# Beginning two weight units of each late run early in the feed-forward output of an encoder trunk

## The chip, the cores and the metric

The kernel runs on one core of a Trainium2 chip. The metric is the device time of one execution in microseconds (us), lower is better, given as the median of several runs. Engines are named as in the profile: PE is TensorE (matmuls; PEld are its weight loads), DVE is VectorE, ACT is ScalarE, POOL is GpSimd, SP is SyncE, whose queue issues the DMA transfers here.

## The reference

The program computes two layers of an encoder trunk on 512 tokens of 1024 channels. Each layer has a half-step SwiGLU feed-forward, a token mixer (neighbourhood attention in the first layer, a bidirectional RWKV-7 scan in the second) and another half-step feed-forward, each followed by a residual sum and a layer norm. The change touches only the feed-forward:

```
def swiglu(x, w_in, w_out):
    gate, up = jnp.split(x @ w_in, 2, axis=-1)
    return (jax.nn.silu(gate) * up) @ w_out
...
x = layer_norm(DN_ALPHA * x + 0.5 * swiglu(x, ffn_w_in[i, 0], ffn_w_out[i, 0]), ln_g[i, 0], ln_b[i, 0])
```

w_in is 1024 x 5632 and w_out 2816 x 1024, all float32. There are four such layers in the program; below they are called the first, second, third and last.

## The kernel before

**Split products.** A float32 product is made of three matmuls: every operand is split into a high part (`h`, a copy that rounds, on ACT, line 220) and a low part (`l`, the value minus the high part, a subtraction on DVE or POOL, line 221), and high x high, high x low and low x high are summed in PSUM. So each weight unit needs a DMA into a raw buffer, a copy on ACT and a subtraction on DVE or POOL before all of its matmuls can run. The matmul with the high half needs only the copy.

**The output product as a Winograd scheme.** The product with w_out is computed by class `Winograd` (line 753), which replaces eight block products by seven. The 22 chunks of 128 hidden channels form 11 pairs, numbered c = 0 to 10. While the projections of pair after pair run, `sums` makes sums of blocks of w_out, writes two of them (t3 and t4) to a DRAM buffer `late`, and the products X, Z and Y of pair c are accumulated early (`early`, matmuls shown as bank<-wx,an). Four more runs over all 11 pairs follow, made by `add` (matmuls shown as bank<-w,ring or bank<-wl,ring):

- V with block b21 of w_out, pairs 0 to 6 and then 7 to 10;
- t3 into the banks of Y, b22 into the banks of Z, and t4 again into the banks of Y: the three late runs.

A run has 11 pairs x 2 row tiles x 3 matmuls = 66 matmuls. A weight unit holds two pairs (c and c + 1, 128 x 2 x 1024 values after the split), the last one, c=10, holds one. It is loaded by `load` (line 812), when `add` comes to an even c.

**Order of the late runs.** After V the outer function `ffn` opens a pool "fo", makes the 14 additions of X, Y, Z and V into the residual x (`more`, line 446, shown as DVE L448), calls `add` for t3, adds Y for rows 2 and 3, calls `add` for b22, then `done(0)` and `done(1)` (the last addition and the normalisation of rows 0 and 1, lines 359 to 369, then transposes, line 328), then `add` for t4, and the ending of rows 2 and 3. In b22 the pairs from 8 on, and in t4 those from 6 on, are lagging: all of them for row tile 0 first, then all for row tile 1 (`lag`, line 843), so that the first tile is finished sooner.

**Buffers.** A split unit goes into one of three buffers of tag `w`; a unit of lagging pairs into a buffer of its own in the pool "fo": `wl2` (two buffers, units of two pairs) or `wl1` (one buffer, c=10). The trace calls both wl. A `w` or `wl` buffer is free again when PE has done the last matmul that reads it. The raw buffers: the first three loads of a layer take the common raw buffers, the later ones eight quarters of two tiles named `late`, in turn, and, where the next stage takes its input as an XT tile (first and second layer), t4's loads take four buffers `rw`, because the tiles `late` lie in the buffers that the new xT then needs (`out.raws = None`, line 478). Counted over a layer the loads are numbers 0 to 5 for V, 6 to 11 for t3, 12 to 17 for b22 and 18 to 23 for t4; number n takes quarter n % 4 of tile n // 4 % 2.

The low part goes to POOL for c = 0, 4 and 8, and to DVE for c = 2, 6 and 10 (line 828).

**What sets the order.** Outside the hand-ordered sections a planner puts the instructions of each engine in a fixed order at build time: among those that its clock holds ready, the one traced first goes first. On the chip each engine, and SP's queue too, then runs its list in order, and an instruction that waits holds up all behind it. `mark` puts a small copy on POOL, and `behind` queues the next stage's first splits on POOL after it (`ending`, line 252).

Of the kernel before, what the change touches and what calls it, by code (L numbers as in the profile page):

```python
# [86 lines left out]
def halves_of(ap):  # L87
    return ap.rearrange("p (h t) -> p h t", h=2)
# [10 lines left out]
class Trunk:  # L99
    def __init__(self, ctx, tc):  # L100
        self.tc = tc
        self.nc = tc.nc
        self.ex, self.spare = None, []
        self.spares = self.nth = None
        nc = self.nc
        self.const = ctx.enter_context(tc.tile_pool(name="const", bufs=1))
        self.ident = self.const.tile([P, P], F32, name="ident")
        make_identity(nc, self.ident)
        self.eps = self.const.tile([P, 1], F32, name="eps")
        nc.gpsimd.memset(self.eps, LN_EPS)  # L110
        self.marks = self.const.tile([P, 1], F32, name="marks")
# [283 lines left out]
    def ffn(self, xT, w_in, w_out, ln, nxt, lead=None):  # L395

        nc = self.nc
        npairs = NF // 2
        params = self.ln_params(ln)
        out = Winograd(self, w_out)
        with self.pool("fa") as pool:
            out.pool = pool
            keep = [self.ring().rearrange("p (i n s) -> p i n s", i=2, n=4) for _ in range(npairs)]
            for c in range(npairs):
                out.sums(c)  # L410
                raw = pool.tile([P, 8, 256], F32, name="ar", tag="ar", bufs=1)
                for j in range(2):
                    f = 2 * c + j
                    if f == 0:
                        pps = self.follow()
                    elif f >= LEAD // 2:
                        pps = [self.proj_cols(self.load_cols(w_in, FF * i + f * P), xT) for i in range(2)]
                    pg, pu = pps.pop(0), pps.pop(0)
                    s = self.tmp()
                    nc.scalar.activation(s, pg, AF.Silu)  # L420

                    nc.vector.scalar_tensor_tensor(raw[:, 3:7:3] if j else raw[:, 0:8:7], halves_of(pu), 0.5, halves_of(s),  # L422
                                                   ALU.mult, ALU.mult)
                    if j == 0 and c:
                        out.early(c - 1)
                a = lambda n: raw[:, n]
                nc.vector.tensor_tensor(a(1), a(7), a(6), ALU.add)
                nc.vector.tensor_tensor(a(2), a(1), a(0), ALU.subtract)
                nc.gpsimd.tensor_tensor(a(4), a(0), a(7), ALU.subtract)
                nc.gpsimd.tensor_tensor(a(5), a(3), a(2), ALU.subtract)  # L430
                out.now[c] = pool.tile([P, 2, 3, 256], F32R, name="an", tag="an", bufs=1)
                self.split(out.now[c][:, 0], out.now[c][:, 1], raw[:, 0:3])
                self.split(keep[c][:, 0], keep[c][:, 1], raw[:, 3:7])
            out.keep = keep
            late = npairs - 4
            out.raws = [self.sb.tile([P, 4 * D], F32, name="late", tag="xT", bufs=2) for _ in range(2)]
            out.add("V", 0, out.b21, range(0, late))
            out.early(npairs - 1)
            out.add("V", 0, out.b21, range(late, npairs))
        nxt = nxt()  # L440
        with self.pool("fo") as pool:
            out.pool = pool
            fin = self.residual_norm(params, nxt)
            hs = (slice(0, 512), slice(512, 1024))

            def more(t, h, acc, scale=1.0, sm=None):
                y = self.x[t][:, hs[h]]
                nc.vector.scalar_tensor_tensor(y, y, scale, acc[t % 2], ALU.mult, ALU.add, accum_out=sm)  # L448

            X, Y, Z, V = (out.acc[n] for n in "XYZV")  # L450
            st = [self.small("st", 5) for _ in range(NT)]
            for t in (0, 1):
                more(t, 1, Y, ALPHA)
            for t in (2, 3):
                more(t, 1, Z, ALPHA)
            for t in (0, 1):
                more(t, 1, X)
            for t in (2, 3):
                more(t, 1, X)
                more(t, 0, X, ALPHA)  # L460
            for t in (0, 1):
                more(t, 0, X, ALPHA)
                more(t, 0, V, 1.0, st[t][0])
            out.add("Y", 1, out.t3, range(npairs))
            for t in (2, 3):
                more(t, 1, Y, 1.0, st[t][1])
            out.add("Z", 2, out.b22, range(npairs), lag=8)

            def done(t):
                h, acc = (1, Z) if t < 2 else (0, Y)  # L470
                more(t, h, acc, 1.0, st[t][h])
                fin(t, st[t])

            done(0)
            done(1)
            mid = nxt and self.mark(self.x[1][:, 0:1])
            if isinstance(nxt, XT):
                out.raws = None
            out.add("Y", 3, out.t4, range(npairs), lag=6)
            if isinstance(nxt, XT):  # L480

                def start(t):
                    more(t, 0, Y, 1.0, st[t][0])
                    return fin(t, st[t], True)

                self.ending(start, lead, nxt, (mid,), (mid,))
            elif nxt:
                self.mid = mid
                with self.tc.manual_schedule(engines=MANUAL_NORM):
                    more(2, 0, Y, 1.0, st[2][0])  # L490
                    n2 = fin(2, st[2], True)
                    for _ in range(3):
                        next(n2)
                    more(3, 0, Y, 1.0, st[3][0])
                    n3 = fin(3, st[3], True)
                    for n in (n3, n3, n3, n2, n3):
                        next(n)
            else:
                done(2)
                done(3)  # L500
        return nxt
# [251 lines left out]
class Winograd:  # L753


    def __init__(self, k, w):
        self.k, self.nc = k, k.nc
        self.w = w.rearrange("(c j p) f -> p c j f", j=2, p=P)
        self.late = k.late
        self.units, self.now, self.acc, self.loads = {}, {}, {}, 0  # L760

    def sums(self, c):

# [48 lines left out]
    def load(self, src, c, lag):  # L812
        k = self.k
        n = min(2, NF // 2 - c)
        if self.loads < 3:
            raw = k.raw()
        elif self.raws:
            raw = self.raws[self.loads // 4 % 2][:, self.loads % 4 * D : self.loads % 4 * D + D]
        else:
            raw = self.pool.tile([P, D], F32, name="rw", tag="rw", bufs=4)  # L820
        self.loads += 1
        raw = raw[:, : n * 512]
        k.nc.sync.dma_start(raw.rearrange("p (c f) -> p c f", c=n), src(c, n))
        if lag:
            u = self.pool.tile([P, 2, n * 512], F32R, name=f"wl{n}", tag=f"wl{n}", bufs=n)
        else:
            u = k.sb_w.tile([P, 2 * D], F32R, name="w", tag="w", bufs=k.nw)[:, : 2 * n * 512].rearrange("p (i f) -> p i f", i=2)
        k.split(u[:, 0], u[:, 1], raw, k.nc.vector if c % 4 else k.nc.gpsimd)
        return u

    def add(self, name, n, src, cs, lag=None):

        first = self.banks(name)
        step = lambda c, t: self.product(self.acc[name][t], self.keep[c], n, t, us[c], first and c == 0, c == NF // 2 - 1, name != "V")
        us = {}
        for c in cs:
            if c % 2 == 0:
                self.duo = self.load(src, c, lag is not None and c >= lag)
            us[c] = self.duo[:, :, c % 2 * 512 : c % 2 * 512 + 512]
            if lag is None or c < lag:  # L840
                for t in range(2):
                    step(c, t)
        if lag is not None:
            for t in range(2):
                for c in range(lag, NF // 2):
                    step(c, t)
# [130 lines left out]
class Scan:  # L977
# [53 lines left out]
    def receptances(self):  # L1031
# [13 lines left out]
        for hp, i in zip(WR_FIRST, (4, 5, 6, 7)):  # L1045
            load(hp, one(self.units[i][0]))
            if hp == 1:
                for c in range(ND):
                    nc.sync.dma_start(self.xv[:, c, :], self.dram["xv"][:, c, :])
# [643 lines left out]
```

## Time and profile before

| | |
|---|---|
| median of 3 runs | 2267.66 us (2266.18 to 2270.35) |
| the profiled execution | 2262.09 us |
| its span (first to last instruction) | 2260.3 us |
| mean granted TensorE clock | 0.984 |
| DMA | 328.82 MB, mean 145 GB/s |

A row of a timeline gives start and length in us, engine, line, operation, what it writes and reads, the shape, how many instructions are merged, and in brackets the idle time of the engine before it with what ended that. In the view by stages a row gives a stretch, its length, the busy time (and count) of PE, PEld, DVE, ACT and POOL, the granted clock, the DMA share and GB/s. In the waits "<-" names the one waited for. "issue" is time in which the engine waited for nothing that the profile shows. The late runs of the four layers, from the first matmul of V, begin at 300.69, 890.27, 1243.63 and 2185.33 us of the profiled span.

### The profile page before, as it was taken

Reading aid. Unit: us, or ns where it says so; the run is one execution under the profiler, and the core shown is the slowest. Engines: PE = TensorE matmul, PEld = TensorE weight load, DVE = VectorE, ACT = ScalarE, POOL = GpSimd, SP = SyncE. Lnnn points to the kernel's source line nnn. Section 1 sums busy time; section 2 is a strip of 40 time slices with the busy share of each in tenths; the row PEclk is TensorE's granted clock in tenths of the full one; section 3 lists DMA queues with packets and bytes.
Section 4 is the critical chain, followed back from the end, with each engine's and each line's share of the span. In section 5 each row is a group of like instructions: output and inputs, shape, how many; then the busy total and the mean of one; then the engine's idle time right before and its main releaser. Section 6 shows DMA issues by size and latency. Waiting matters only on the chain. (4 is left out here: it accounts for less than half of the span.)

```text
span 2260.3 us, 35130 instructions
## 1 busy us (share of the span) xinstructions
PE 2169.9 (96%) x13784; PEld 1707.2 (76%) x13784; DVE 1084.6 (48%) x1549; ACT 974.6 (43%) x1706; POOL 1423.4 (63%) x1237
## 2 busy tenths in 40 slices
PE   8999999999999999999999988799999898999998
PEld 7888878887888888788888775435666556888886
DVE  2333356376423333743333698435787535233346
ACT  4333335376333333533333436336777533333334
POOL 6878855554487886588777433144776712888763
PEclk9999999999999999999999999899999999999999
DMA  7444463432344445354444534864444542444443
GB/s 204 143 149 145 140 214 101 134 89 91 103 140 149 144 141 181 123 176 140 140 140 134 192 122 143 275 165 132 134 125 119 181 149 85 158 144 140 145 168 121
DMA packets 350497, 328.82 MB, mean 145 GB/s; under 512 B 48458, under 2 KB 277450, under 8 KB 350332
## 3 DMA queue, kind: packets, MB, share of 16 engines
q1 hardware_dynamic: 350332, 326.58, 45.9%
q8 instruction: 108, 1.77, 0.3%
q14 instruction: 57, 0.47, 0.1%
HBM read 262.26 MB, written 47.74 MB: 137 GB/s over the span
## 5 line engine op out<-in xcount | busy, mean ns | idle before, releaser
L221 POOL TENSOR_TENSOR w<-raw,w 128x1024 fp32r<-128x1024 f32 (+2 forms) x203 | 501.5, 2472 | 253.6 <-ACT w L220 240.1
L226 PE MATMUL bank<-xT,w 128*128 128x512 f32 x1416 | 551.8, 390 | 1.7 <-DVE xT L221 1.7
L225 PE MATMUL bank<-xT,w 128*128 128x512 f32 x1416 | 552.9, 390 | 0.0
L227 PE MATMUL bank<-xT,w 128*128 128x512 f32 x1416 | 551.5, 389 | 0.0
L220 ACT ACTIVATE w<-raw 128x1024 fp32r<-128x1024 f32 x207 | 218.4, 1058 | 327.9 <-POOL ts L768 138.0
L422 DVE SCALAR_TENSOR_TENSOR ar<-bank,tmp 128x512 f32<-128x512 f32 x88 | 60.9, 692 | 580.7 <-PE bank L227 566.2
L226 PEld LDWEIGHTS bank<-xT,w 128*128 128x128 f32 x1416 | 266.1, 188 | 56.6 <-DVE xT L221 2.6
L227 PEld LDWEIGHTS bank<-xT,w 128*128 128x128 f32 x1416 | 266.0, 188 | 54.9
L225 PEld LDWEIGHTS bank<-xT,w 128*128 128x128 f32 x1416 | 266.0, 188 | 54.0
L797 PE MATMUL bank<-w,ring 128*128 128x512 f32 x864 | 201.5, 391 | 11.0 <-DVE w L221 10.1
L797 PEld LDWEIGHTS bank<-w,ring 128*128 128x128 f32 x864 | 161.6, 188 | 48.3 <-DVE w L221 13.1
L797 PE MATMUL bank<-wx,an 128*128 128x512 f32 x792 | 187.3, 389 | 0.0
L1360 POOL TENSOR_TENSOR tm<-qs,zs 128x126 f32<-128x126 f32 (+22 forms) x248 | 105.5, 425 | 125.7 <-DVE qs L1353 77.3
L797 PEld LDWEIGHTS bank<-wx,an 128*128 128x128 f32 x792 | 148.8, 188 | 30.8
L221 POOL TENSOR_TENSOR wx<-ra,wx 128x512 fp32r<-128x512 f32 x132 | 166.8, 1291 | 3.5 <-ACT wx L220 2.4
L221 DVE TENSOR_TENSOR ring<-ar,ring 128x1024 fp32r<-128x1024 f32 x44 | 130.0, 2955 | 76.0 <-ACT ring L220 75.9
L420 ACT ACTIVATE tmp<-bank 128x512 f32<-128x512 f32 x88 | 52.6, 598 | 225.8 <-PE bank L227 225.7
L221 POOL TENSOR_TENSOR ring<-raw,ring 128x1024 fp32r<-128x1024 f32 x28 | 69.7, 2499 | 105.6 <-ACT ring L220 105.6
L1362 POOL TENSOR_TENSOR zs<-zs,tm 128x126 f32<-128x126 f32 (+22 forms) x248 | 112.2, 452 | 19.4
L221 POOL TENSOR_TENSOR w<-late,w 128x1024 fp32r<-128x1024 f32 x28 | 71.3, 2547 | 75.9 <-ACT w L220 68.9
L220 ACT ACTIVATE wx<-ra 128x512 fp32r<-128x512 f32 x132 | 82.9, 633 | 72.4 <-PE bank L797 67.9
L225 PE MATMUL bank<-xT,ring 128*128 128x256 f32 (+1 forms) x352 | 104.5, 304 | 9.5 <-ACT xT L220 3.4
(285 smaller groups left out, 3730.5 us busy)
## 6 DMA issues: line engine op xcount, KB each, us to landing
raw<-in_ffn_w_in_dram SPq DMA_DIRECT2D x176, 512.0 KB, 3.7
ra<-in_ffn_w_out_dram SPq DMA_DIRECT2D x44, 1024.0 KB, 4.9
late<-d_late SPq DMA_DIRECT2D x30, 512.0 KB, 6.0
late<-in_ffn_w_out_dram SPq DMA_DIRECT2D x28, 512.0 KB, 4.4
raw<-in_w_qkv_dram SPq DMA_DIRECT2D x24, 512.0 KB, 3.8
d_late<-ts SPq DMA_DIRECT2D x44, 256.0 KB, 3.1
d_late<-ra SPq DMA_DIRECT2D x44, 256.0 KB, 2.0
xs<-ar SPq DMA_DIRECT2D x64, 128.0 KB, 2.3
```

What stands on the lines that cost most here:

```text
L220: self.hi = self.nc.scalar.activation(h, raw, AF.Copy).ins
L221: self.lo = (eng or self.nc.vector).tensor_tensor(l, raw, h.bitcast(F32), ALU.subtract).ins
L225: nc.tensor.matmul(out, wh, xh, start=start, stop=False)
L226: nc.tensor.matmul(out, wh, xl, start=False, stop=False)
L227: nc.tensor.matmul(out, wl, xh, start=False, stop=stop)
L420: nc.scalar.activation(s, pg, AF.Silu)
L422: nc.vector.scalar_tensor_tensor(raw[:, 3:7:3] if j else raw[:, 0:8:7], halves_of(pu), 0.5, halves_of(s), ALU.mult, ALU.mult)
L797: self.nc.tensor.matmul(acc, lhs, u[:, i], start=bool(first) and m == 0, stop=last and m == 2, skip_group_check=more)
L1360: nc.gpsimd.tensor_tensor(tv, qs[:, s, 0:s].rearrange("p (a o) -> p a o", o=1).broadcast_to([P, s, n]), zs[:, s : s + 1, c0:].broadcast_to ...
L1362: nc.gpsimd.tensor_tensor(zs[:, 0:s, c0:], zs[:, 0:s, c0:], tv, ALU.add)
```

## The change

A new method `begin` loads the units c=0 and c=2 of a run ahead of time and keeps them in a table; `add` takes them from there. It is called for t3 as soon as the pool "fo" is open, ahead of the additions; for b22 after t3's products, ahead of the additions of Y to rows 2 and 3; and for t4 after b22's products, ahead of the normalisation of rows 0 and 1 and ahead of `out.raws = None`, so that in the first two layers t4's first two loads use quarters of `late` and only its other four use `rw`. The order of the loads among themselves stays the same. And the unit c=2 of each late run is put into a buffer `wl2` instead of one of `w`: wl2's two buffers now serve, in this order, t3's c=2, b22's c=2 and c=8, and t4's c=2, c=6 and c=8; before they served b22's c=8 and t4's c=6 and c=8.

```
@@ ffn
         with self.pool("fo") as pool:
             out.pool = pool
+            out.begin(out.t3)
             fin = self.residual_norm(params, nxt)
...
             out.add("Y", 1, out.t3, range(npairs))
+            out.begin(out.b22)
             for t in (2, 3):
                 more(t, 1, Y, 1.0, st[t][1])
             out.add("Z", 2, out.b22, range(npairs), lag=8)
+            out.begin(out.t4)
@@ Winograd.load
-        if lag:
+        if lag or c == 2 and src != self.b21:
             u = self.pool.tile([P, 2, n * 512], F32R, name=f"wl{n}", tag=f"wl{n}", bufs=n)
@@ Winograd
+    def begin(self, src):
+        for c in (0, 2):
+            self.begun[src.__name__, c] = self.load(src, c, False)
@@ Winograd.add
             if c % 2 == 0:
-                self.duo = self.load(src, c, lag is not None and c >= lag)
+                now = (src.__name__, c)
+                self.duo = self.begun.pop(now) if now in self.begun else self.load(src, c, lag is not None and c >= lag)
```

More of the change, by code (lines that the diff above doesn't have):

```diff
@@ L442, in ffn @@
             out.pool = pool
+            out.begin(out.t3)
             fin = self.residual_norm(params, nxt)
@@ L464, in ffn @@
             out.add("Y", 1, out.t3, range(npairs))
+            out.begin(out.b22)
             for t in (2, 3):
@@ L467, in ffn @@
             out.add("Z", 2, out.b22, range(npairs), lag=8)
+            out.begin(out.t4)
             def done(t):
@@ L759, in __init__ @@
         self.late = k.late
-        self.units, self.now, self.acc, self.loads = {}, {}, {}, 0
+        self.units, self.now, self.acc, self.loads, self.begun = {}, {}, {}, 0, {}
     def sums(self, c):
@@ L823, in load @@
         k.nc.sync.dma_start(raw.rearrange("p (c f) -> p c f", c=n), src(c, n))
-        if lag:
+        if lag or c == 2 and src != self.b21:
             u = self.pool.tile([P, 2, n * 512], F32R, name=f"wl{n}", tag=f"wl{n}", bufs=n)
@@ L829, in load, with begin @@
         return u
+    def begin(self, src):
+        for c in (0, 2):
+            self.begun[src.__name__, c] = self.load(src, c, False)
     def add(self, name, n, src, cs, lag=None):
@@ L837, in add @@
             if c % 2 == 0:
-                self.duo = self.load(src, c, lag is not None and c >= lag)
+                now = (src.__name__, c)
+                self.duo = self.begun.pop(now) if now in self.begun else self.load(src, c, lag is not None and c >= lag)
             us[c] = self.duo[:, :, c % 2 * 512 : c % 2 * 512 + 512]
```

## The prediction

> **What bounds the kernel now.** I read the page first, then the timeline of PE through the end of each of the four feed-forward layers, then the timelines of VectorE (DVE), GpSimd (POOL) and ScalarE (ACT) at the places where PE stood still. From the page:
>
> ```profile
> PE 2169.9 (96%) x13784; PEld 1707.2 (76%) x13784; DVE 1084.6 (48%) x1549; ACT 974.6 (43%) x1706; POOL 1423.4 (63%) x1237
> ```
>
> TensorE carries the time, so an edit that leaves its work alone can gain only where it idles. The edit touches the end of the feed-forward layers (V, the early products, then the late runs t3, b22 and t4). The timeline of PE there (start, length, count, and in brackets the idle time before and what ended it), first layer:
>
> ```profile
> 300.69 6.06 PE L797 MATMUL bank<-w,ring 128*128 128x512 f32 x26
> ...
> 314.29 8.78 PE L797 MATMUL bank<-w,ring 128*128 128x512 f32 x38
> 324.65 12.53 PE L797 MATMUL bank<-w,ring 128*128 128x512 f32 x54 [1.58 <-DVE w L221]
> 337.72 3.01 PE L797 MATMUL bank<-w,ring 128*128 128x512 f32 x12 [0.54 <-POOL w L221]
> 341.61 8.03 PE L797 MATMUL bank<-w,ring 128*128 128x512 f32 x34 [0.88 <-DVE w L221]
> 349.47 4.24 PE L797 MATMUL bank<-wl,ring 128*128 128x512 f32 x18
> 353.55 8.32 PE L797 MATMUL bank<-w,ring 128*128 128x512 f32 x36
> ...
> 363.75 1.03 PE L328 MATMUL bank<-ident,x 128*128 128x128 f32 x8
> 364.54 5.93 PE L797 MATMUL bank<-wl,ring 128*128 128x512 f32 x25
> ```
>
> The first row gives the pace: 26 matmuls in 6.06 us, the last taking 0.39, so one starts every (6.06 - 0.39) / 25 = 0.227 us. From it to the row of 353.55 (the first of t4) the program has 66 + 18 + 66 + 66 = 216 matmuls (the three matmuls of a split product, by two row tiles, by eleven chunks for V, t3 and b22; 18 early ones), 49.0 us at that pace. The view by stages gives the length of this stretch in each of the four layers, then what PE was busy:
>
> ```profile
> 300.70:353.50 52.80, 49.80 (x217) 40.31 (x216) 34.31 (x39) 22.32 (x23) 26.76 (x11) 1.00 0.58 202
> 890.30:942.90 52.60, 49.78 (x217) 40.31 (x216) 34.57 (x39) 22.28 (x23) 26.62 (x11) 1.00 0.57 202
> 1243.60:1297.00 53.40, 49.64 (x218) 40.45 (x217) 33.20 (x41) 22.30 (x23) 26.23 (x11) 1.00 0.56 199
> 2185.30:2236.50 51.20, 49.74 (x217) 40.46 (x216) 31.41 (x39) 22.42 (x23) 27.23 (x11) 1.00 0.54 188
> ```
>
> Over 49.0 the first three lose 3.8, 3.6 and 4.4 us. In the first they are the three stops of the timeline, 1.58, 0.54 and 0.88, and the other 0.8 is some 0.3 of restart at each. The third and the last layer have other stops:
>
> ```profile
> 1267.59 11.18 PE L797 MATMUL bank<-w,ring 128*128 128x512 f32 x48 [1.58 <-DVE w L221]
> 1280.94 12.11 PE L797 MATMUL bank<-w,ring 128*128 128x512 f32 x52 [2.18 <-DVE w L221]
> ```
>
> ```profile
> 2220.33 12.14 PE L797 MATMUL bank<-w,ring 128*128 128x512 f32 x52 [1.46 <-DVE w L221]
> ```
>
> The last has one stop, 1.46 + 0.3 = 1.8. Together 3.8 + 3.6 + 4.4 + 1.8 = **13.6 us**: this is all that the edit can win there.
>
> **Part by part.**
>
> *Unit c=2 of t3.* What ends the stop at 324.65 is the subtraction (the low half of a split weight) of that unit:
>
> ```profile
> 312.03 1.10 DVE L221 TENSOR_TENSOR w<-late,w 128x512 fp32r<-128x512 f32 x1 [3.50 <-ACT w L220]
> 313.36 7.86 DVE L448 SCALAR_TENSOR_TENSOR x<-x,bank 128x512 f32<-128x512 f32 x13 [0.23 <-PE bank L797]
> ...
> 321.15 3.45 DVE L221 TENSOR_TENSOR w<-late,w 128x1024 fp32r<-128x1024 f32 x1
> ```
>
> ```profile
> 321.12 2.38 POOL L221 TENSOR_TENSOR w<-late,w 128x1024 fp32r<-128x1024 f32 x1 [1.73 <-issue]
> ```
>
> It stands behind 13 additions (L448), and then takes 3.45 us because POOL began unit c=4 just before it. In the last layer the same pair met the other way round, and no stop followed:
>
> ```profile
> 2205.78 1.22 DVE L221 TENSOR_TENSOR w<-late,w 128x1024 fp32r<-128x1024 f32 x1
> ```
>
> ```profile
> 2205.92 3.36 POOL L221 TENSOR_TENSOR w<-late,w 128x1024 fp32r<-128x1024 f32 x1 [1.83 <-issue]
> ```
>
> So 1.22 is its price alone. After the edit its split is asked for ahead of the additions, into wl2, which no late weight holds then, so no matmul of V has to free it. Its source was fetched early:
>
> ```profile
> 298.58 1.41 SPq L823 DMA_DIRECT2D late<-d_late  x3
> ```
>
> ```profile
> DMA to landing us min/median/max: 3.3/5.4/9.5
> ```
>
> The first late loads left by 300.0 and are there by 309.5 at worst. ACT's copy (1.06 us, the rows of w<-late) and DVE's 1.22 fit into the 3.50 us that DVE idles up to 312.03, or just ahead of the additions; PE wants the unit at 314.29 + 38 x 0.227 = 322.9. If the copy waits at the head of ACT's queue, V's last two copies stand behind it, but PE uses their units only after 314.29. Wholly in the additions' way it delays them by 1.2 us (2.4 more if POOL is just ahead); t3's first product, 24 matmuls after 314.29 or at 319.7, needs only the first two, done by 314.8. So it costs nothing while that cover of 5 us lasts. The slot of w that the unit leaves lets c=4 to c=8 be split a turn (12 matmuls, 2.7 us) sooner. Gain 1.9 us in each of the first three layers.
>
> *Units c=0 and c=2 of b22.* What ends the other two stops:
>
> ```profile
> 331.92 2.40 POOL L221 TENSOR_TENSOR wl<-late,wl 128x1024 fp32r<-128x1024 f32 x1 [1.15 <-ACT wl L220]
> 334.34 3.33 POOL L221 TENSOR_TENSOR w<-late,w 128x1024 fp32r<-128x1024 f32 x1
> ```
>
> ```profile
> 335.33 2.88 DVE L221 TENSOR_TENSOR wl<-late,wl 128x512 fp32r<-128x512 f32 x1
> ...
> 338.75 2.81 DVE L221 TENSOR_TENSOR w<-late,w 128x1024 fp32r<-128x1024 f32 x1
> ```
>
> b22's first unit waits on POOL for its own lagging unit c=8; its second waits on DVE behind the lagging c=10 and an addition. The second goes to wl2's other buffer; its source buffer is one of V's last, free at 312.03 + 1.10 = 313.1, and lands 5.4 later, at about 319, long before PE needs it at 341: that stop, 0.88 + 0.3, goes. The first unit still needs a slot of w that t3's c=7 frees, so asking earlier buys little by itself; c=8, its rival on POOL, does come earlier, since t3's c=4 leaves its source buffer 2.7 us sooner. I take half of that stop as gone.
>
> *The last units of t3* make the stop of 2.18 in the third layer and of 1.46 in the last:
>
> ```profile
> 1275.64 2.48 DVE L221 TENSOR_TENSOR wl<-late,wl 128x512 fp32r<-128x512 f32 x1 [6.37 <-ACT wl L220]
> 1278.04 2.84 DVE L221 TENSOR_TENSOR w<-late,w 128x512 fp32r<-128x512 f32 x1
> ```
>
> Unit c=10 of t3 follows b22's c=10 on DVE, each slowed by POOL beside it. b22's lagging source is requested when t3's c=4 and c=6 have been split. That comes about 2.7 us sooner while PE, without its first stop, wants c=10 only 1.9 sooner, so most of this goes too. But the same order can now arise in the first two layers. By these rows a unit of half width, 0.6 us alone by the 1.22 for a whole one, took 2.84: the loser of such a meeting is late by 2.2 us; I take one meeting in four, 0.5 per layer.
>
> The Trainium skill (SBUF — State Buffer, "Who interferes with whom") says that a DVE instruction with two SBUF inputs and a GpSimd one never share their port pair: whoever starts first holds it to its end. The trace agrees: 3.45 beside 2.38, and 1.22 beside 3.36. By it, the 0.5 above stands; were the port shared, both would only slow a little, and the sum would come out some 2 us lower.
>
> *t4.* c=0 and c=2 are asked for ahead of the normalisations of rows 0 and 1, with sources in the old "late" buffers where the next stage takes xT. On SP they wait until t3's c=8 and c=10 are split, which PE itself needs before t3 ends (337.72); behind them stand t4's other loads, needed after 353.55, and the next stage's. Fetched even 9.5 us after that, nothing is late. But wl2 now carries six units in two buffers, and t4's c=6, until now split during t3, must wait for b22's c=8 to be used up (just before 353.55, call it E); c=8 waits for t4's c=2 and c=3, 24 matmuls or 5.4 us after E. Before:
>
> ```profile
> 353.84 1.56 ACT L220 ACTIVATE wl<-rw 128x1024 fp32r<-128x1024 f32 x2
> ```
>
> ```profile
> 354.96 2.40 POOL L221 TENSOR_TENSOR wl<-rw,wl 128x1024 fp32r<-128x1024 f32 x1 [1.75 <-ACT wl L220]
> ...
> 362.23 4.74 POOL L221 TENSOR_TENSOR ring<-raw,ring 128x1024 fp32r<-128x1024 f32 x2
> ```
>
> ```profile
> 360.81 1.42 DVE L369 SCALAR_TENSOR_TENSOR x<-tmp,st,bbc 128x512 f32<-128x512 f32 x2
> ```
>
> c=6 then has its copy at E + 0.3 to 1.3 and 1.2 us on DVE, against a need at 36 matmuls, E + 8.2. c=8 has its copy from E + 5.5 to 6.5 (7.5 with another copy ahead) and is done on POOL 2.4 later, at E + 10 at the latest, against a need at the eighth lagging matmul: E + 8.2 + 7 x 0.227 = 9.8 without transposes between (the last layer), 364.54 + 0.45 or E + 11.4 with them. Both hold, the last layer's by a hair. What they take is DVE time under the normalisations: 1.2 us more, against 363.75 - 362.23 = 1.5 us by which row 1's x is ready before its transposes. I charge 0.3 in the first three layers and 0.2 in the last (bounds 0 and 1.2).
>
> **The sum**, in us. First layer 3.8, less 0.4 (half of 0.54 + 0.3), 0.5 and 0.3: 2.6. Second 3.6 less 1.2: 2.4. Third 4.4 less 0.5 and 0.3: 3.6. Last 1.8 less 0.5 and 0.2: 1.1. Together 9.7. After each layer PE goes on from its own end, so this reaches the end of the program. The profiled execution took 2262.09 (span 2260.3, 1.8 around it) and would take 2252.4; the median of the runs is 5.6 above it, 2267.66, and falls to **2258.0**.
>
> **Rivals.** (1) *The stop moves to the end of t3 or to b22's first unit*: the meeting of DVE and POOL happens in every layer. For it: DVE and POOL are both busy from 331 to 341. Against it: with three units fewer on w they have more time. It leaves the whole 2.2 in place of my 0.5 in the first three layers, 5.1 more, 1.1 in the last (it has 1.8 in all, 0.7 of it charged), and in the first two the other half of the stop at b22, 0.4 each: 7.0 back, 2265.0.
>
> (2) *Slower: t4's c=8 lands behind the next stage's weights.* If the planner puts POOL's mark and the two ring subtractions ahead of it, it starts when they end, 366.97 or E + 13.4, ends at E + 15.8, and PE, needing it at E + 11.4, stops 4.4 us. That is 13.2 in the three layers that have such weights: 2258.0 + 13.2 = 2271.2. It decides once c=8's subtraction starts after E + 9.0. Against it: its copy can be done at E + 6.5, the mark waits for row 1's x (360.81, or E + 7.3, at the earliest), and t4 is traced ahead of the next stage.
>
> (3) *It does not do what it says*: the planner issues by readiness, so both c=2 subtractions could still follow the additions and meet POOL as before, with only the slots moved. Then 1.9 in three layers and 1.2 in two stay: 8.1 of the 9.7, 2266.1. Against it: both would be ready long before.
>
> **Chances.** 0.2% is 4.5 us, about what a measurement here can tell from no change. Forecast 0.67 (2252 to 2262), rival 1 0.16, rival 2 0.10, rival 3 0.07. Faster by over 0.2% (below 2263.1): the forecast and half of rival 1, which can come in part, 0.75. Within: the other half, rival 3, and 0.04 of rival 2, whose price is near the bound: 0.19. Slower: 0.06. The range starts at 2252, with all 13.6 gone (2254.1) and 2 us of the spread of the runs before, and reaches 2267, past rivals 1 and 3; rival 2 is left out.
>
> **What would show it.** Right: no idle row of PE inside t3 after its first 14 matmuls, c=2's subtraction of 1.2 us ahead of the run of L448, the four stretches to t4 at 49.5 to 50 us. Wrong: a stop before t4's lagging rows (wl) or before the transposes, ended by POOL wl or DVE; a stop at t3's last unit in the first two layers; or stretches that shrink while the span does not.

## The result, and the profile after

| | before | after |
|---|---|---|
| median (4 runs each) | 2269.01 us (2266.18 to 2270.53) | 2252.74 us (2249.58 to 2256.88) |
| the profiled execution | 2262.09 us | 2249.58 us |
| its span | 2260.3 us | 2247.8 us |

The ratio is 0.993, with a 95% interval of 0.9913 to 0.9948: about 16 us faster, between 12 and 20. The lines of after.py are one to three higher than before's in the feed-forward (L448 is L449, L797 is L800, L823 is L826) and eight higher in the scan.

The view by stages of after, from the first matmul of V to the first of t4 in each of the four layers (length, then busy time and count of PE, PEld, DVE, ACT, POOL):

```profile
301.62:350.57 48.95, 48.95 (x218) 40.54 (x216) 31.61 (x39) 21.21 (x22) 25.87 (x11) 1.00 0.62 219
887.45:936.51 49.06, 49.06 (x217) 40.47 (x216) 34.16 (x39) 21.14 (x22) 26.89 (x11) 1.00 0.62 217
1237.23:1286.90 49.67, 49.28 (x217) 40.46 (x216) 30.08 (x41) 21.43 (x22) 26.27 (x11) 1.00 0.62 215
2171.80:2223.26 51.46, 49.72 (x218) 40.44 (x216) 30.21 (x39) 21.23 (x22) 27.39 (x11) 1.00 0.54 186
```

The first two layers have reached the 49.0 us at which PE never stops (PE is busy for the whole length), the third is 0.7 above it, and the last is longer than before (51.20). PE's timeline in after's first layer shows the same without one idle time in brackets:

```profile
315.21 8.32 PE L800 MATMUL bank<-w,ring 128*128 128x512 f32 x36
323.37 2.88 PE L800 MATMUL bank<-wl,ring 128*128 128x512 f32 x12
326.09 12.40 PE L800 MATMUL bank<-w,ring 128*128 128x512 f32 x54
338.33 2.88 PE L800 MATMUL bank<-wl,ring 128*128 128x512 f32 x12
341.05 5.60 PE L800 MATMUL bank<-w,ring 128*128 128x512 f32 x24
346.49 4.24 PE L800 MATMUL bank<-wl,ring 128*128 128x512 f32 x18
```

The two rows of 12 matmuls with wl are the units c=2 of t3 and of b22. What is left in after are two stops at places where before had none, one in the third layer (at b22's first unit) and one in the last (at t3's first unit), both ended by POOL:

```profile
1272.22 2.60 PE L800 MATMUL bank<-w,ring 128*128 128x512 f32 x10 [0.39 <-POOL w L221]
...
2193.34 2.56 PE L800 MATMUL bank<-w,ring 128*128 128x512 f32 x10 [1.74 <-POOL w L221]
```

**Where the 12.5 us between the two spans went.** Lengths in us between the starts of PE's first matmul of each run; the last two columns are the way from the last matmul of t4 to the next layer's V (for the last layer, to the end of the span):

| layer | t3 before, after | b22 before, after | t4 before, after | way on before, after |
|---|---|---|---|---|
| first | 16.83, 14.96 | 16.99, 14.96 | 16.53, 16.53 | 520.19, 520.35 |
| second | 16.84, 14.96 | 16.79, 15.07 | 16.52, 16.53 | 284.17, 284.18 |
| third | 19.31, 14.96 | 14.98, 15.68 | 16.52, 16.53 | 871.85, 868.36 |
| last | 16.84, 17.15 | 15.13, 15.12 | 14.89, 14.90 | 8.90, 9.63 |

The late runs give 3.9, 3.6 and 3.6 us in the first three layers and take 0.3 in the last, whose ending takes another 0.7: 10.1 together. Another 3.5 us come from a place that the diff doesn't touch, the 870 us between the third and the last layer, where the scan is. The way from the start of the program to the first V is 0.9 longer, and that behind the first layer 0.2. 3.9 + 3.6 + 3.6 - 0.3 - 0.7 + 3.5 - 0.2 - 0.9 = 12.5.

**The scan.** SP issues there five loads of the output weights, one behind the other. Its timeline in before:

```profile
1786.90 0.55 SPq L1484 DMA_DIRECT2D xs<-in_rw_out_dram  x1
1787.55 0.40 SPq L1482 DMA_DIRECT2D bk<-in_rw_out_dram  x1
1788.00 0.42 SPq L1484 DMA_DIRECT2D xs<-in_rw_out_dram  x1
1788.63 0.33 SPq L1473 DMA_DIRECT2D ar<-in_rw_out_dram  x1
1789.05 0.59 SPq L1473 DMA_DIRECT2D wv<-in_rw_out_dram  x1
```

and in after:

```profile
1783.65 0.54 SPq L1490 DMA_DIRECT2D bk<-in_rw_out_dram  x1
1784.27 0.41 SPq L1481 DMA_DIRECT2D wv<-in_rw_out_dram  x1
1784.74 0.43 SPq L1492 DMA_DIRECT2D xs<-in_rw_out_dram  x1
1785.38 0.33 SPq L1481 DMA_DIRECT2D ar<-in_rw_out_dram  x1
1785.76 0.44 SPq L1492 DMA_DIRECT2D xs<-in_rw_out_dram  x1
```

wv, which PE needs first, has moved from the fifth place to the second. PE's rows that wait for it, before and then after:

```profile
1797.72 1.98 PE L982 MATMUL a<-wv,xv 128*64 128x512 f32 x4 [5.79 <-DMA wv<-in_rw_out_dram]
```

```profile
1788.89 1.98 PE L990 MATMUL a<-wv,xv 128*64 128x512 f32 x4
```

From issue to use it is 8.7 us in the fifth place and 4.6 in the second, and PE's stop of 5.79 is gone. So the planner, which lays out the whole program, has given the scan another order, although the change is elsewhere. What this is worth had to be measured by itself. A few copies and subtractions on ACT and DVE, between 1347 and 1377 us, stand in another order too; no run tests these alone.

### The profile page after: what moved, and what is told of

It reads as the page before. It is cut to its first block, busy times and chain, and to the rows that moved or that the text cites. A ratio compares the mean times of both kernels' runs of the same rounds, so it can differ in the third digit from the quotient of the medians.

```text
span 2247.8 us, 35130 instructions
## 1 busy us (share of the span) xinstructions
PE 2169.0 (96%) x13784; PEld 1707.8 (76%) x13784; DVE 1068.3 (48%) x1549; ACT 973.8 (43%) x1706; POOL 1425.7 (63%) x1237
## 4 chain that ended last, share of the span: by engine, by line
PE 83%; DVE 7%; DMA 4%; ACT 3%; issue 2%; POOL 1%; SPq 0%; DVEq 0%; ACTq 0%; POOLq 0%
PE bank L800 16%; PE bank L225 16%; PE bank L226 16%; PE bank L227 16%; PE bank L288 4%; PE a L990 3%; PE y L990 1%; PE g L1279 1%; DVE tmp L606 1%; PE m L990 1%; PE bank L1155 1%; DMA late<-in_ffn_w_out_dram 1%; PE g L990 1%; POOL w L221 1%; DMA wv<-in_w_rkv_dram 1%
## 5 line engine op out<-in xcount | busy, mean ns | idle before, releaser
L221 POOL TENSOR_TENSOR w<-raw,w 128x1024 fp32r<-128x1024 f32 (+2 forms) x203 | 507.2, 2500 | 248.3 <-ACT w L220 235.2
L800 PE MATMUL bank<-wx,an 128*128 128x512 f32 x792 | 187.3, 389 | 0.0
L800 PEld LDWEIGHTS bank<-wx,an 128*128 128x128 f32 x792 | 148.7, 188 | 30.8
L800 PE MATMUL bank<-w,ring 128*128 128x512 f32 x720 | 168.8, 390 | 2.1 <-POOL w L221 2.1
L221 DVE TENSOR_TENSOR ring<-ar,ring 128x1024 fp32r<-128x1024 f32 x44 | 122.8, 2792 | 81.3 <-ACT ring L220 81.2
L800 PEld LDWEIGHTS bank<-w,ring 128*128 128x128 f32 x720 | 134.9, 188 | 31.5 <-POOL w L221 3.2
```

Source lines behind the costliest of these rows:

```text
L221: self.lo = (eng or self.nc.vector).tensor_tensor(l, raw, h.bitcast(F32), ALU.subtract).ins
L800: self.nc.tensor.matmul(acc, lhs, u[:, i], start=bool(first) and m == 0, stop=last and m == 2, skip_group_check=more)
```

## The experiments

My theory: a unit c=2 with a buffer of its own is split as soon as its transfer has landed, and so the stops go one by one, each with its own unit. Rivals: the earlier tracing (`begin`) does the work; or the new tile simply relieves the three w buffers, whichever unit takes it; and, for the scan, that its gain belongs to one execution.

### The same program again, and each half of the change alone

The control is before with blank lines, so that its lines match:

> The kernel before, unchanged but for blank lines. Its ratio to the kernel before shows what a difference of nothing measures as: 0.998 to 1.002. The stretches from V to t4 should repeat those of the profile before (52.9, 52.7, 53.3, 51.2 us) within 0.2, since each stop comes from a fixed order of instructions. If the 3.5 us that the profile of the changed kernel gained between the third and the last layer are chance (waits of the scan for DMA), this run's stretch there (871.9 before, 868.4 after) differs from 871.9 by a few us with nothing changed; if they belong to the change, it stays at 871.9.

After again:

> The changed kernel again. Theory that the gain is the stops of PE in the first three layers (3.9 + 3.6 + 3.6 less 0.3 to 1.0 lost in the last layer): 10 to 11 us, ratio 0.995 to 0.9955. Theory that something outside the layers gained 3 to 6 us besides: 0.993, as in the first comparison.

The buffer alone, without the calls of `begin`:

```
-            out.begin(out.t3)
...
-            out.begin(out.b22)
...
-            out.begin(out.t4)
```

> The units c=2 of the late runs in wl2, but no run begun early. Theory that the buffer does it: the stretches fall as in the changed kernel (49.0, 49.1, 49.7, 51.5 us), the last layer's stop of 1.7 us is there too, ratio 0.994 to 0.9955. Rival, that the early beginning does it: stops of 1.5 us in t3 stay, stretches of 52 us and more, ratio 0.998 to 1.

`begin` alone, with c=2 in w as before:

```
-        if lag or c == 2 and src != self.b21:
+        if lag:
```

> The runs begun early, but c=2 in the buffers of w as before. Theory that the buffer does it: a unit asked for earlier still waits for the slot that V's last units hold, so the stops stay: stretches of 52.5 to 53.3 in the first three layers, 51.2 in the last, ratio 0.998 to 1.001. Rival, that the early beginning does it: stretches of 49 to 50, ratio 0.995.

Each kernel from here on is compared with before on the same chip. Measured against before's 2266.55 us: the control 2267.82, ratio 1.0007 [0.9998, 1.0015]; after 2248.91, 0.9929 [0.9915, 0.9944]; the buffer alone 2247.38, 0.9921 [0.9908, 0.9934]; `begin` alone 2270.0, 1.0014 [1.0002, 1.0026].

So the buffer does it all. With it alone, t3 takes 14.96 us in the first three layers and 17.15 in the last, the same as after to 0.06 us, and b22 at most 0.4 us more. `begin` alone gains nothing: in its first layer PE's timeline has the stop at t3's c=2 as before, and in place of those at b22 one at the end of t3:

```profile
326.06 11.17 PE L800 MATMUL bank<-w,ring 128*128 128x512 f32 x48 [1.58 <-DVE w L221]
339.98 13.71 PE L800 MATMUL bank<-w,ring 128*128 128x512 f32 x52 [2.75 <-DVE w L221]
```

t3 is 19.87 us long there and b22 16.60, against 16.83 and 17.01 in the control. The stop at the end of t3 is that of its c=10: on ACT and on DVE the planner has put t4's c=6 ahead of it, whose subtraction takes 2.59 us there. In the third and the last layer `begin` leaves every queue in the order of before.

That b22 still takes 16.60 us, though it has no stop, is another effect: for some 3.4 us behind the stop the granted clock is 0.5 (half clock, below) and the matmuls start 0.43 us apart in place of 0.227, which costs 1.6 us. The control shows the same in its third layer, where b22 takes 16.60 us against 14.98 in the profile before, after a stop of 1.94 us in t3 (2.18 in the profile before). Its view by stages, in the slow stretch and just after it:

```profile
1285.00:1288.40 3.40, 3.40 (x10) 2.63 (x9) 2.13 (x5) 1.06 (x1) 2.09 (x1) 0.50 0.94 322
1288.40:1291.80 3.40, 3.40 (x16) 2.79 (x15) 1.16 (x2) 2.01 (x2) 0.36 (x1) 1.00 0.84 275
```

The late runs of all profiles have six such stretches, each behind a stop of 1.9 to 2.8 us; five other stops of 1.9 to 2.4 us, and all shorter ones, have none. No run shows what decides it. So the length of a run can differ by 1.6 us between two executions of the same kernel, and the tables here have to be read with the stops beside them.

### The buffer for one run at a time

In before, each with one condition in place of `if lag`:

```
-        if lag:
+        if lag or c == 2 and src == self.t3:
```

> Before, with the new tile for t3's second weight unit alone; nothing is begun earlier. Theory that each unit's own place in the queue counts: t3's stretch falls from 16.8 to 15.0 in the first two layers and from 19.1 to about 17 in the third, b22's stretch keeps its 1.7 to 2 us of stops: -5.8 us. Rival, that the new tile relieves the two w buffers for whatever comes next: b22's stops go as well, -10 us. On the scan's end: in this kernel SP issues the load of wv from the output weights ahead of those of xs, as in after; if that order is worth its 5 us, the wait of 5.6 us for wv is gone and the sums are -10 to -11 (own place) or -15 (relief), about 2257 or 2252; if the scan's gain was only one execution's, -6 or -10.

```
+        if lag or c == 2 and src == self.b22:
```

> Before, with the new tile for b22's second weight unit alone. Own place: b22's stretch falls from 17.0 to about 15.3 in the first two layers and keeps about 0.5 us of its first unit's stop; t3 keeps its 1.9 us stop in each: -3.4 us, or -5 if the third layer's b22 is the longer one. Relief of the w buffers: t3 cannot gain from it either, since it comes first, so the two agree here, unless t3's third split meets it (then t3 is 1 to 2 us longer and nothing is gained). SP's order at the scan's end is that of before in this kernel: if the order is the cause, the wait of 5.6 us for wv stays; if the new tile brings the scan's gain in another way, it goes, with some 5 us more.

```
+        if lag or c == 2 and src == self.t4:
```

> Before, with the new tile for t4's second weight unit alone. Own place: no stop of t3 or b22 goes, no stop stands in t4 either way, so the late runs hold before's lengths within 0.3 us each; the end after the last late run is 0.7 us longer, 9.63 for 8.89, because t4's last split is later there. SP has after's order at the scan's end, worth 5 us. Sum -4 to -5 us, about 2262, ratio 0.998. Rival, that t4's part is what frees the two w buffers for b22's last units: b22 falls to 15 us in the first two layers, 4 us more, ratio 0.996.

| buffer for | ratio to before | t3 in the four layers | b22 in the four layers |
|---|---|---|---|
| none (control) | 1.0007 [0.9998, 1.0015] | 16.83, 16.84, 19.06, 17.00 | 17.01, 17.08, 16.60, 15.13 |
| t3 | 0.9926 [0.9911, 0.9942] | 14.96, 14.96, 14.96, 15.12 | 16.93, 16.95, 14.96, 15.12 |
| b22 | 1.0008 [0.9997, 1.002] | 19.49, 17.33, 18.97, 19.07 | 14.96, 14.96, 14.96, 15.12 |
| t4 | 1.0017 [1.0005, 1.003] | 16.83, 16.84, 20.26, 16.78 | 17.31, 17.21, 18.11, 20.30 |

t3's buffer alone is worth as much as the whole change. It takes all of t3's stops and leaves b22's in the first two layers, so the theory of relief for all falls. That of one unit, one stop holds for b22's stops and is too narrow for t3's: the stops at c=10 go as well, and the third layer's t3 takes 14.96 us where 17 were expected. In before c=10's subtraction ran beside one of POOL there and took 2.84 us; with t3's buffer it takes 0.68:

```profile
1271.01 0.68 DVE L221 TENSOR_TENSOR w<-late,w 128x512 fp32r<-128x512 f32 x1
```

(b22's 16.60 in the third layer of the control is the half clock, not a stop.) PE's timeline with t3's buffer alone, at b22 of the first layer, still has the two stops of before:

```profile
336.37 3.06 PE L800 MATMUL bank<-w,ring 128*128 128x512 f32 x12 [0.50 <-POOL w L221]
340.26 8.01 PE L800 MATMUL bank<-w,ring 128*128 128x512 f32 x34 [0.84 <-DVE w L221]
```

But the theory failed for the other two. b22's buffer alone clears b22 wholly and puts the time back into t3, 2.7 us in the first layer. There b22's c=2 now stands on DVE ahead of t3's, and t3's subtraction then starts beside one of POOL; DVE, POOL and PE of that kernel:

```profile
324.27 2.78 DVE L221 TENSOR_TENSOR w<-late,w 128x1024 fp32r<-128x1024 f32 x1
```

```profile
323.00 2.98 POOL L221 TENSOR_TENSOR w<-late,w 128x1024 fp32r<-128x1024 f32 x1 [2.18 <-issue]
```

```profile
327.11 16.41 PE L800 MATMUL bank<-w,ring 128*128 128x512 f32 x64 [2.63 <-DVE w L221]
```

DVE ends 1.07 us after POOL does, which is about the 1.2 us that such a subtraction takes alone, as if it had got nothing done before. The stop is only 1.05 us longer than in before (2.63 for 1.58); the other 1.6 of the 2.7 us are matmuls at a granted clock of 0.5, from 328.1 to 331.5. And t4's buffer alone loses 4 us where 4 to 5 were to be gained: it makes b22 longer, in the last layer by 5.2 us. ACT's timeline there:

```profile
2229.79 1.06 ACT L220 ACTIVATE wl<-late 128x1024 fp32r<-128x1024 f32 x1 [7.36 <-DMA late<-d_late]
2230.76 2.93 ACT L220 ACTIVATE w<-late 128x1024 fp32r<-128x1024 f32 x3
```

The copy of t4's unit has a free buffer, so the planner puts it early; on the chip its transfer is not there, ACT waits 7.36 us with it at the head of its queue, and three copies for b22, which PE wants first, stand behind it. PE stops there for 1.93 us on ACT's copy and for 1.32 on the subtraction after it, and some 1.5 us more go to matmuls at half clock.

### The last layer

After's own stop of 1.74 us in the last layer looks the same. ACT's timeline of after:

```profile
2183.00 1.04 ACT L220 ACTIVATE wl<-late 128x1024 fp32r<-128x1024 f32 x1
2188.50 1.06 ACT L220 ACTIVATE wl<-late 128x1024 fp32r<-128x1024 f32 x1 [4.45 <-issue]
2189.46 2.93 ACT L220 ACTIVATE w<-late 128x1024 fp32r<-128x1024 f32 x3
```

The first row is t3's c=2, the second b22's c=2, and only then come three copies into w, the first of them t3's c=0. The row names no cause of the 4.45 us, but the transfer of b22's c=2 landed at 2188.43, just before the copy began. POOL can begin on t3's c=0 at 2190.58. The edit puts b22's early copies behind it:

```
@@ ffn
-            out.begin(out.b22)
+            with self.behind(out.turn):
+                out.begin(out.b22)
@@ Winograd.load
         k.split(u[:, 0], u[:, 1], raw, k.nc.vector if c % 4 else k.nc.gpsimd)
+        if src == self.t3 and c == 0:
+            self.turn = k.hi
```

> After, with one order added: on ACT's queue b22's first two copies stand behind t3's first copy. The stop of 1.74 us in the last layer's t3 came, I think, because b22's second copy stood first in ACT's queue and waited 4.45 us for its transfer. If so, t3 of the last layer goes from 17.15 us to about 15.1, the other layers stay, and the kernel is 1.5 to 2 us faster than after (about 2247 beside before's 2267, ratio near 0.9920). Rival: t3's first weight unit is late of itself there (its transfer, or POOL's lagging rows), or its third split meets b22's: t3 stays at 17 and the time at 2249, ratio 0.9929.

Measured: 2246.97 us against before's 2266.64, ratio 0.9917 [0.9901, 0.9933]. ACT's timeline in the last layer, and PE's:

```profile
2191.77 1.06 ACT L220 ACTIVATE w<-late 128x1024 fp32r<-128x1024 f32 x1 [2.95 <-PE bank L801]
2192.89 1.06 ACT L220 ACTIVATE wl<-late 128x1024 fp32r<-128x1024 f32 x1
```

```profile
2190.17 8.47 PE L801 MATMUL bank<-w,ring 128*128 128x512 f32 x36
2198.48 2.88 PE L801 MATMUL bank<-wl,ring 128*128 128x512 f32 x12
```

The two copies have changed places, the stop is gone and t3 takes 15.12 us there. Apart from them only b22's c=10, further on in the last layer, stands in another place on ACT and DVE than in after: the cause is settled. In this kernel t3 and b22 are within 0.03 us of their shortest lengths in all four layers. The ratio to before overlaps that of after, so the 2 us are shown by the profile and not by the times.

### The order at the scan's end

In before, first the two loads of xs alone put behind that of wv, so that wv is third of the five; then, with a second order for ar, wv second as in after. Every other instruction of SP, and every one of ACT, DVE and POOL, keeps the order of before. The diff is the second kernel's; the first lacks the `with` at i == 2.

```
@@ Scan.outs
         for i in range(EARLY - 1):
             nc.sync.dma_start(self.xv[:, i, :], self.dram["o"][:, i, :])
-            nc.sync.dma_start(w[i], rows(self.w_out, i))
+            with self.k.behind(*(dmas if i == 2 else [])):
+                dma = nc.sync.dma_start(w[i], rows(self.w_out, i))
+            dmas = [dma.ins] if i == 0 else dmas
...
-                    for c in range(EARLY, ND - 1):
-                        nc.sync.dma_start(w[c], rows(self.w_out, c))
+                    with self.k.behind(dmas[0]):
+                        for c in range(EARLY, ND - 1):
+                            nc.sync.dma_start(w[c], rows(self.w_out, c))
```

> Before, with one thing changed at the scan's end: SP issues the two xs loads of the output weights behind the wv load and not ahead of it; every other instruction stands where it stood. If this order is what gave after 3 to 8 us between its third and last layer, the wait of 5.6 us of PE for wv falls to under 2 us and the kernel is 3 to 5 us faster than before, about 2263 (ratio 0.998). If the scan's gain came from elsewhere, or the other loads are then as late as wv was, the ratio is 1.000 within 0.001 and the wait only changes its name.

> Before, with wv's load from the output weights in the second place of the five such loads that SP issues at the scan's end, the place that it has in after (before has it last; putting it ahead of the two xs loads alone left 3.0 us of the 5.6 us wait). Every other instruction stands as in before. If SP's order is the whole cause of the scan's gain, PE's wait for wv falls to under 1 us and the kernel gains 4.5 to 5.5 us: 2262, ratio 0.998, with the four late runs as in before. Rival: the rest of the gain comes with the new tile's programs in some other way, or the load that goes last is now what PE waits for: ratio 0.999 to 1.000, or a wait of 3 us for ar.

Measured: wv third, 2262.71 against 2266.64, ratio 0.9989 [0.9978, 1.0001], which is not clear of no change; wv second, 2263.18 against 2266.12, 0.9981 [0.997, 0.9992]. PE's wait in the one and in the other:

```profile
1797.62 1.97 PE L990 MATMUL a<-wv,xv 128*64 128x512 f32 x4 [3.02 <-DMA wv<-in_rw_out_dram]
```

```profile
1796.32 1.98 PE L990 MATMUL a<-wv,xv 128*64 128x512 f32 x4 [0.86 <-DMA wv<-in_rw_out_dram]
```

5.8 us in the fifth place, 3.0 in the third (under 2 was expected), 0.9 in the second: the wait follows the order alone. By the ratio the order of after is worth 4.3 us (1.8 to 6.8). The other kernels agree. Before, the control, `begin` alone and b22's buffer alone have wv last, and wait 5.4 to 5.8 us for it; all others with a buffer have it second, and wait 0.8 or less. The rest of the difference between the third and the last layer scatters from one execution to the next: 864.3 to 872.1 us among the eight profiles with wv second, 869.9 to 872.9 among the four with wv last. Their means, 867.7 and 871.9, are 4.2 apart, as the ratio has it.

### Without t4's buffer

Since t4's c=2 loses nothing in w, the last kernel leaves it there, and keeps the order on ACT:

```
-        if lag or c == 2 and src != self.b21:
+        if lag or c == 2 and src in (self.t3, self.b22):
```

> After with b22's early copies behind t3's first on ACT, and without the new tile for t4's second unit (t3's and b22's keep it). If t4's part only costs, t3 and b22 keep 15.0 in all layers, t4 its 16.5 and 14.9, and the end after the last late run goes from 9.63 to 8.89: 0.7 us less than with t4's part, about 2246, ratio 0.9913 to 0.992. Rival: t4's second unit, back in a w buffer, holds up b22's last units or t4's later ones: 1 to 2 us more in each of the first three layers, 2250.

Measured: 2248.26 us against 2266.12, ratio 0.9919 [0.9902, 0.9936]. t3 takes 14.96, 14.96, 14.96 and 15.12, b22 14.96, 14.96, 15.27 and 15.12, t4 as before, and the way from t4's last matmul to the end is 8.89 us again where after has 9.63. Its profiled execution has the shortest span of all, 2241.7 us. That it is faster than after is read from these lengths (2.1 + 0.7 us); the times can't tell it.

## Why the prediction was right, and where it was not

The direction was right, and the median of after, 2252.74 us, lies at the lower end of the range. That it lies inside is partly luck: measured again, after takes 2248.91 us, below the 2252 at which the range starts. The gain of 9.7 us was too small beside the 12 to 20 measured. What it lacked is the scan and not, in the profiled pair, the late runs, which gave 10.1 there; between the control and after measured again they gave 12.6, of which 1.6 are the control's stretch at half clock. The prediction had no term for that clock either. Step by step:

- **t3's c=2, 1.9 us in each of three layers.** Measured 1.87, 1.88 and, with the other stop of the third layer, 4.35. The size was right and its timing failed at one step: "The first late loads left by 300.0 and are there by 309.5 at worst." The three loads of that row are numbers 8 to 10 (c=4, 6 and 8), which take the first `late` tile. c=2 is number 7, in the other tile, which leaves in the pair after it. SP's timeline of after, and ACT's:

```profile
299.50 1.41 SPq L826 DMA_DIRECT2D late<-d_late  x3
...
303.82 1.09 SPq L826 DMA_DIRECT2D late<-d_late  x2
```

```profile
313.71 1.06 ACT L220 ACTIVATE wl<-late 128x1024 fp32r<-128x1024 f32 x1 [0.80 <-DMA late<-d_late]
```

  It lands at 313.7, so the subtraction can't stand ahead of the additions, as "What would show it" had it. DVE's timeline of after has it behind nine of the thirteen:

```profile
314.52 5.46 DVE L449 SCALAR_TENSOR_TENSOR x<-x,bank 128x512 f32<-128x512 f32 x9
319.90 1.51 DVE L221 TENSOR_TENSOR wl<-late,wl 128x1024 fp32r<-128x1024 f32 x1
321.33 1.87 DVE L449 SCALAR_TENSOR_TENSOR x<-x,bank 128x512 f32<-128x512 f32 x3
```

  It ends at 321.41 and PE uses it at 323.37: four additions sooner was enough, with 2 us to spare and not the 5 of the prediction. The cause is the buffer: in before ACT copies this unit later, when PE has freed a slot of w.
- **b22's two stops, 1.2 and half of 0.8.** Both went in the first two layers (2.0 and 1.7 us); the charge of 0.4 was too careful there. In the third layer before had no stop in b22; there 0.39 is new and b22 is 0.7 longer, which no term had. After measured again has no stop there and 15.05 us, so this one comes and goes between executions.
- **t3's c=10, less 0.5 for a meeting of DVE and POOL.** The stop went altogether in the third layer. Meetings occur in after as well: its c=6 of t3 takes 2.94 us on DVE, from 325.30 to 328.24, beside POOL's 324.76 to 327.16. DVE ends 1.08 us after POOL, as the rule of the Trainium skill that the prediction used (SBUF — State Buffer, "Who interferes with whom") would have it. PE stopped at none of them, so the 0.5 was not spent.
- **The last layer, 1.1 us.** This term failed, and has the other sign: 0.3 us are lost in the late runs, where the stop of 1.46 at c=10 went and one of 1.74 at c=0 came; the stretch to t4 is 51.46 us where the prediction's sign of being right had 49.5 to 50. The prediction let a copy wait at the head of ACT's queue and named who stands behind it, but only for t3's copy and V's last units. The one that waited was b22's, and t3's first unit was behind it.
- **t4, 0.3 in three layers and 0.2 in the last.** In the first three layers it cost nothing. POOL's timeline of after, with the mark in the second row:

```profile
358.28 2.86 POOL L221 TENSOR_TENSOR wl<-rw,wl 128x1024 fp32r<-128x1024 f32 x1 [10.71 <-ACT wl L220]
361.09 0.18 POOL L377 COPY marks<-x 128x1 f32<-128x1 f32 x1
```

  c=8 ends at E + 10.6 (E is 350.57, t4's first matmul), 0.6 later than the latest that was reckoned, and no stop follows. In the last layer the cost came behind t4: 0.7 us, within the bounds (0 and 1.2). DVE's timeline of after shows the last additions of the two tiles:

```profile
2236.73 0.69 DVE L449 SCALAR_TENSOR_TENSOR x<-x,bank 128x512 f32<-128x512 f32 x1 [3.29 <-PE bank L800]
...
2239.04 0.68 DVE L449 SCALAR_TENSOR_TENSOR x<-x,bank 128x512 f32<-128x512 f32 x1
```

  They come 5.3 us after the first lagging matmul (2231.42) and 2.3 apart, in before 3.7 and 4.1: the first tile is finished later and its normalisation is in the second's way.
- **Rival 1** (the stop moves to the end of t3 or to b22's first unit) came in after only as the 0.39 us of the third layer; `begin` alone moves one to the end of t3, and b22's buffer alone makes those of t3 longer. **Rival 2** (c=8 behind the next stage's weights) fell: c=8's subtraction stands ahead of the mark. **Rival 3** was half right: the planner does go by readiness, so that tracing earlier gained nothing by itself, but a free buffer makes a unit ready.
- **What no step had.** The scan's order, 4.3 us. The prediction took it that an edit in the feed-forward leaves the rest of the program as it is. Why the planner's clock comes out so that wv goes second with t3's or t4's buffer, and last with b22's alone, was not followed.

## What to carry to other kernels

Where a planner orders the work by readiness, a buffer of its own for one unit can do what tracing that unit earlier does not; but a unit with a free buffer can also be put ahead of others before its transfer has landed, and then it holds up the queue that it stands in. Try such buffers one at a time and say with an explicit order who goes first. After any edit compare the order of every queue in the whole program, not only at the edit: here about a quarter of the gain came from a queue some 390 us ahead of the last layer's V, in code that the edit doesn't touch. And look at the granted clock before a longer run is put down to a wait.

## What had not been expected of the hardware

Five loads of the same size (128 x 1024 float32), issued within some 3 us, differ by their place. In before they land in the order of their issue, 3.7, 4.9, 5.7, 6.6 and 8.6 us after it. wv lands 4.6 to 5.0 us after its issue in the second place (eight profiles), 6.3 in the third (one) and 8.0 to 8.6 in the fifth (four), and PE uses it within 0.1 us. That is 1.0 to 1.3 us more for each place, as if the loads landed one after the other; so the order on the queue decides which consumer waits.

A stop of PE of 1.9 to 2.8 us can cost more than its length: in six cases of eleven the granted clock was 0.5 for some 3.4 us behind it, 1.6 us more. What decides it stays open.
